# An interleaving copy without its small early write to the output

## The chip, the cores and the metric

One core of a Trainium2 chip runs the kernel. The metric is the device time of one execution in microseconds (us). Times quoted are medians of several executions. A ratio is computed otherwise: the mean time of one kernel's fast runs over the mean of the other's fast runs of the same rounds, so it is not quite the ratio of the medians.

## The reference

```python
# x, y: (32, 256, 1024) float32
result = np.zeros((batch, seq, dim * 2), dtype=np.float32)
result[..., 0::2] = x
result[..., 1::2] = y
```

Nothing is computed: 33.55 MB of x and as much of y are read, and 67.11 MB of output is written with the elements of the two inputs in turn.

## The kernel before

The kernel walks over 8 pairs of tiles of 128 partitions x 8192 elements (4 MB each). x and y are loaded from the SP queue; the vector engine copies x to the even and y to the odd places of an output tile, in halves of 4096 columns; the ACT queue stores each half (4 MB). Every pool has two buffers. The first x tile is loaded in two halves, one from each queue. Then comes the part that the change is about.

```python
xpool = ctx.enter_context(tc.tile_pool(name="xp", bufs=2))
ypool = ctx.enter_context(tc.tile_pool(name="yp", bufs=2))
opool = ctx.enter_context(tc.tile_pool(name="op", bufs=2))
# ... (cut)
wpool = ctx.enter_context(tc.tile_pool(name="wp", bufs=1))
zero = wpool.tile([16, 128], fp32, name="zero")
nc.vector.memset(zero, 0.0)
first = dataclasses.replace(of, offset=0, ap=[[2 * WL, 16], [1, 128]])

for lw in lwidths:                      # 8 times, lw = WL = 8192
    # ... (cut: xtile, ytile, xs, ys)
    if start == 0:
        for q, c in ((nc.sync, 0), (nc.scalar, lw // 2)):
            q.dma_start(out=xtile[:, c : c + lw // 2], in_=...)   # half of x
        nc.scalar.dma_start(out=first, in_=zero)                  # the small write
    else:
        nc.sync.dma_start(out=xtile, in_=xs)
    nc.sync.dma_start(out=ytile, in_=ys)
    # ... (cut: for each half of WS = 4096 columns)
        nc.vector.tensor_copy(out=otile[:, 0::2], in_=xsub)
        nc.vector.tensor_copy(out=otile[:, 1::2], in_=ysub)
        nc.scalar.dma_start(out=os_, in_=otile)
```

The small write puts 16 rows of 512 B of zeros, 8 KB in all, at places of the output that the first store overwrites later. It contributes nothing to the result.

Of the kernel before, what the change touches and what calls it, by code (L numbers as in the profile page):

```python
# [3 lines left out]

# [4 lines left out]


@with_exitstack
def _interleave(
    ctx: ExitStack,
    tc: tile.TileContext,
    x: bass.AP,
    y: bass.AP,
    out: bass.AP,
):
    nc = tc.nc  # L20
    P = 128

    total = 1
    for s in x.shape:
        total *= s

    WL = 8192
    WS = 4096

    xf = x.rearrange("b s d -> (b s d)")  # L30
    yf = y.rearrange("b s d -> (b s d)")
    of = out.rearrange("b s d -> (b s d)")

    fp32 = mybir.dt.float32
# [5 lines that stand above are left out]
    lwidths = [WL] * (total // P // WL)  # L40
    assert sum(lwidths) == total // P


    wpool = ctx.enter_context(tc.tile_pool(name="wp", bufs=1))
    zero = wpool.tile([16, 128], fp32, name="zero")
    nc.vector.memset(zero, 0.0)  # L46
    first = dataclasses.replace(of, offset=0, ap=[[2 * WL, 16], [1, 128]])

    start = 0
    for lw in lwidths:  # L50
        xtile = xpool.tile([P, WL], fp32, name="xtile")[:, :lw]
        ytile = ypool.tile([P, WL], fp32, name="ytile")[:, :lw]

        xs = dataclasses.replace(xf, offset=start, ap=[[lw, P], [1, lw]])
        ys = dataclasses.replace(yf, offset=start, ap=[[lw, P], [1, lw]])
        if start == 0:

            for q, c in ((nc.sync, 0), (nc.scalar, lw // 2)):
                q.dma_start(
                    out=xtile[:, c : c + lw // 2],  # L60
                    in_=dataclasses.replace(xf, offset=c, ap=[[lw, P], [1, lw // 2]]),
                )
            nc.scalar.dma_start(out=first, in_=zero)
        else:
            nc.sync.dma_start(out=xtile, in_=xs)
        nc.sync.dma_start(out=ytile, in_=ys)

        soff = 0
        while soff < lw:
            width = min(WS, lw - soff)  # L70
            otile = opool.tile([P, 2 * WS], fp32, name="otile")[:, : 2 * width]
            os_ = dataclasses.replace(
                of,
                offset=2 * start + 2 * soff,
                ap=[[2 * lw, P], [1, 2 * width]],
            )
            xsub = xtile[:, soff : soff + width]
            ysub = ytile[:, soff : soff + width]
# [3 lines that stand above are left out]
            soff += width  # L82

        start += P * lw
    assert start == total


def kernel(tc, x, y, out):
    nc = tc.nc
    _interleave(tc, x, y, out)  # L90
    tc.close()
    tc.compile()  # L92


    blocks = nc.main_func.blocks
    for engine in (mybir.EngineType.SP, mybir.EngineType.Activation):
        opening = blocks[0].instructions
        at, moved = next(
            (b, i)
            for b in blocks[1:]  # L100
            for i in b.instructions
            if i.engine == engine and i.opcode == "DMACopy"
        )
        assert not moved.sync_info.on_wait
        body = at.instructions
        body.remove(moved)
        gate = next(
            n
            for n, i in enumerate(opening)
            if i.engine == engine and i.opcode == "Drain"  # L110
        )
        opening.insert(gate, moved)
        at.instructions = body
        blocks[0].instructions = opening




    last = nc.main_func.blocks[-1]
    tail = last.instructions  # L120
    wait = tail[0]
    clear = next(n for n, i in enumerate(tail) if i.opcode == "ISA")
    assert wait.engine == mybir.EngineType.SP and wait.opcode == "Drain"
    assert wait.sync_info.on_wait and not wait.sync_info.on_update
    assert tail[clear].engine == mybir.EngineType.Pool
    last.instructions = [
        copy.replace(wait, engine=mybir.EngineType.Pool)
    ] + tail[clear:]


# [1 line left out]
_INS = ['x', 'y']  # L132
_OUTS = [((32, 256, 2048), 'float32')]


# [23 lines left out]
```

## Time and profile before

| | before |
|---|---|
| median of 3 runs | 315.84 us (315.67 to 316.25) |
| span of the profiled execution | 313.8 us |
| moved | 134.23 MB, 428 GB/s over the span |
| vector engine busy | 72.8 us (23%) |

The prediction below shows the totals, the rates by stretch and the start. Here is the chain that ended last, in order of time (start, length, what), from the first store on:

```profile
26.59 40.92 DMA out_dram<-otile
67.51 0.03 issue
67.53 0.02 DVEq L79
67.56 0.04 issue
67.60 2.30 DVE otile L79
```

Most of the chain (76% of the span) is a store on its way; the vector engine's 2.3 us pieces lie between. A store takes 13 to 41 us to land (half of them over 29 us) although its 4 MB need 9.7 us at 434 GB/s, because it shares the DMA engines with loads that are queued at the same time. The chain names who waits for whom; what limits the kernel is the sum of the bytes.

One more thing is needed to follow the argument. The trace holds a record of each DMA packet: queue, start, duration, size. In the large transfers a packet is 32 KB (16 KB in the first two half loads). I call *excess* what the records of the large packets in a stretch have over their usual 1213 ns (611 ns for 16 KB), counted where it is more than 12 ns, added up and divided by the 16 engines.

### The profile page before, as it was taken

To read this page: it belongs to the slowest core of one execution; us is meant where nothing else is said; L and a number is where in the kernel's file an instruction comes from. 1 tells how busy PE (TensorE), PEld (TensorE's weight loads), DVE (VectorE), ACT (ScalarE), POOL (GpSimd) and SP (SyncE) were. 2 spreads that over 40 slices of the span, in tenths; PEclk is the share of its full clock that TensorE was granted. 3 is DMA by queue.
4 is the path that set the end of the run, shared out by engine and by line. 5 is a ranking of instruction groups with operands and counts; after the bars stand their busy time and mean duration, and the time that the engine had idled before them with its cause. 6 is when DMAs were issued, how large, how long until landed. Compare 5 with 4: busy or idle time off the path is not lost.

```text
span 313.8 us, 141 instructions
## 1 busy us (share of the span) xinstructions
DVE 72.8 (23%) x33; POOL 0.2 (0%) x4
## 2 busy tenths in 40 slices
DVE  0523002231022410325003150031501305023500
POOL 0000000000000000000000000000000000000000
DMA  8999999999999999999999999999999999999997
GB/s 343 461 414 388 455 414 455 414 455 414 447 422 447 422 430 439 422 447 418 451 414 455 401 468 401 468 401 464 405 455 414 455 414 455 414 455 414 455 414 334
DMA packets 4784, 134.23 MB, mean 428 GB/s; under 512 B 544, under 2 KB 560, under 8 KB 560
## 3 DMA queue, kind: packets, MB, share of 16 engines
q10 hardware_dynamic: 2480, 69.22, 51.1%
q1 hardware_dynamic: 2304, 65.01, 48.4%
HBM read 67.11 MB, written 67.12 MB: 428 GB/s over the span
## 4 chain that ended last, share of the span: by engine, by line
DMA 83%; DVE 11%; DVEq 1%; issue 0%
DMA out_dram<-otile 76%; DMA ytile<-in_y_dram 7%; DVE otile L80 6%; DVE otile L79 5%; DVEq L92 1%; DVEq L79 0%
## 5 line engine op out<-in xcount | busy, mean ns | idle before, releaser
L79 DVE COPY otile<-xtile 128x4096 f32<-128x4096 f32 x16 | 36.6, 2295 | 184.7 <-DMA out_dram<-otile 174.1
L80 DVE COPY otile<-ytile 128x4096 f32<-128x4096 f32 x16 | 36.6, 2291 | 40.0 <-DMA ytile<-in_y_dram 40.0
L46 DVE MEMSET zero<- 16x128 f32 x1 | 0.2, 165 | 1.0 <-PEq L143 1.0
L143 POOL MEMSET const-bfloat16-1.0<- 128x1 bf16 x1 | 0.1, 101 | 0.0
L143 POOL MEMSET const-uint8-127<- 128x1 uint8 x1 | 0.1, 101 | 0.0
L143 POOL MEMSET const-float32-0.0<- 128x1 f32 x1 | 0.1, 98 | 0.2 <-issue 0.2
L143 POOL MEMSET const-float32-1.0<- 128x1 f32 x1 | 0.1, 98 | 0.0
## 6 DMA issues: line engine op xcount, KB each, us to landing
out_dram<-otile ACTq DMA_DIRECT2D x16, 4096.0 KB, 29.1
ytile<-in_y_dram SPq DMA_DIRECT2D x8, 4096.0 KB, 60.8
xtile<-in_x_dram SPq DMA_DIRECT2D x7, 4096.0 KB, 43.6
xtile<-in_x_dram SPq DMA_DIRECT2D x1, 2048.0 KB, 11.7
xtile<-in_x_dram ACTq DMA_DIRECT2D x1, 2048.0 KB, 13.4
out_dram<-zero ACTq DMA_DIRECT2D x1, 8.0 KB, 14.8
```

The lines of the kernel that those rows point to most:

```text
L46: nc.vector.memset(zero, 0.0)
L79: nc.vector.tensor_copy(out=otile[:, 0::2], in_=xsub)
L80: nc.vector.tensor_copy(out=otile[:, 1::2], in_=ysub)
L92: tc.compile()
L143: nc = _bacc.Bacc("TRN2", target_bir_lowering=False, num_devices=1)
```

## The change

Its intent: to leave out work that the result does not need.

```diff
-    wpool = ctx.enter_context(tc.tile_pool(name="wp", bufs=1))
-    zero = wpool.tile([16, 128], fp32, name="zero")
-    nc.vector.memset(zero, 0.0)
-    first = dataclasses.replace(of, offset=0, ap=[[2 * WL, 16], [1, 128]])
...
-            nc.scalar.dma_start(out=first, in_=zero)
```

## The prediction

> **What bounds the kernel now.** I read the page's totals first, then its slices in time, then the chain that ended last, and only then the start-up, because that is where the small write sits. The page of the kernel before, its totals, slices and queues:
>
> ```profile
> span 313.8 us, 141 instructions
> DVE 72.8 (23%) x33; POOL 0.2 (0%) x4
> ...
> DMA  8999999999999999999999999999999999999997
> GB/s 343 461 414 388 455 414 455 414 455 414 447 422 447 422 430 439 422 447 418 451 414 455 401 468 401 468 401 464 405 455 414 455 414 455 414 455 414 455 414 334
> DMA packets 4784, 134.23 MB, mean 428 GB/s; under 512 B 544, under 2 KB 560, under 8 KB 560
> ```
>
> The vector engine, the only engine that computes, is busy 23% of the time. The DMA row is at 9 (90% or more) in every slice but the first and the last. Of the packets, 544 are under 512 B; that is 34 transfers times 16 engines, the semaphore writes that end each transfer. 560 minus 544 leaves 16 packets of at least 512 B and under 2 KB: these are the small write, one packet for each engine. All else is in large packets. So the kernel moves 134.23 MB through 16 engines that hardly ever rest, and its time is bytes over rate plus what is lost at the ends.
>
> How level is that rate? The busy-time view in chosen stretches of the span (columns: stretch and its length, DVE, POOL, granted clock, DMA share, GB/s):
>
> ```profile
> 2.00:12.00 10.00, 0.28 (x1) 0.00 (x0) 1.00 1.05 447
> 12.00:16.00 4.00, 4.00 (x2) 0.00 (x0) 1.00 0.92 395
> 16.00:25.00 9.00, 3.15 (x3) 0.00 (x0) 1.00 1.05 455
> 25.00:29.00 4.00, 1.56 (x1) 0.00 (x0) 1.00 0.86 287
> 29.00:290.00 261.00, 59.00 (x26) 0.00 (x0) 1.00 1.00 434
> 290.00:312.00 22.00, 4.60 (x3) 0.00 (x0) 1.00 0.99 429
> 312.00:313.80 1.80, 0.00 (x0) 0.00 (x0) 1.00 0.01 0
> ```
>
> A packet is booked where it starts and lasts about 1.2 us, so short stretches swing by some 10% (447, 395 and 455 belong together). The reader is to see two things. From 29 to 290 us the engines are full at 434 GB/s. And there is one real dip, 287 GB/s between 25 and 29 us, just when the first large stores are issued. The trace's single packet records sharpen it: the 32 KB packets take 1213 ns nearly everywhere, but those that start between 25 and 28 us take up to 2046 ns, and the excess over 1213 ns adds up to 0.78 us for each engine (75 + 88 + 619 ns). This is the only loss after start-up, and it comes in spite of the small write having gone out before.
>
> The start in order of time:
>
> ```profile
> 1.00 0.17 DVE L46 MEMSET zero<- 16x128 f32 x1 [1.00 <-PEq L143]
> 1.20 0.39 ACTq L63 DMA_DIRECT2D out_dram<-zero  x1
> 1.30 0.52 SPq L65 DMA_DIRECT2D xtile<-in_x_dram  x1
> 1.87 0.47 SPq L66 DMA_DIRECT2D ytile<-in_y_dram  x1
> 11.72 4.50 DVE L79 COPY otile<-xtile 128x4096 f32<-128x4096 f32 x2 [10.55 <-DMA xtile<-in_x_dram]
> 16.24 0.33 SPq L65 DMA_DIRECT2D xtile<-in_x_dram  x1
> 22.06 4.49 DVE L80 COPY otile<-ytile 128x4096 f32<-128x4096 f32 x2 [5.85 <-DMA ytile<-in_y_dram]
> 24.39 2.56 ACTq L81 DMA_DIRECT2D out_dram<-otile  x2
> 26.59 0.33 SPq L66 DMA_DIRECT2D ytile<-in_y_dram  x1
> ```
>
> And the landing time of the small write, from the list of DMA issues:
>
> ```profile
> out_dram<-zero ACTq DMA_DIRECT2D x1, 8.0 KB, 14.8
> ```
>
> **What the Trainium skill says.** "DMA: Bandwidth & Descriptors", section Bandwidth, puts the ceiling of the 16 engines at 435 GB/s; the 434 GB/s of the long stretch agrees, so there is no slack for a smaller program to use. The same page, section Queues, rings and completion order, says each DMA engine takes turns between the queues that have work, a packet at a time. The trace agrees: the data of the small write starts at 13.7 us, and on each engine about 1.2 us passes between it and its semaphore write, the length of one 32 KB packet of the load queue. So the landing of 14.8 us is waiting in line behind loads, not cost. The page's Specifications give 512 B as the least size of a transfer at line rate; the small write's rows are just 512 B, and its packets took 27 ns each in the trace. I found no page that speaks of a first write to memory needing to be warmed; what the small write may have been for rests on the trace alone.
>
> **The change part by part.** Removed on the vector engine: one memset of 0.17 us at 1.00 us. That engine then idles until 11.72 us for x, so this is worth 0. Removed on the ACT queue: one issue of 0.39 us at 1.20 us. The next thing that queue does is the first store at 24.39 us; worth 0. While this issue ran, the SP queue's two neighbouring issues took 0.52 and 0.47 us against 0.33 us later, so they may get some 0.3 us shorter in sum. But they queue behind the first y load, whose data comes in until about 21 us; worth 0.
>
> Removed waits, from the built programs' order of instructions: the first store waited for the small write to land, because both write the same rows, and the second refill of y waited for it because it reuses its semaphore. The small write landed at 1.20 + 14.8 = 16.0 us. The first store was released by the first y copy, 22.06 + 2.29 = 24.35 us, and the refill by the second, at about 26.56 us. Both waits had been satisfied 8 us or more before; worth 0. Without the small write the eight DMA semaphores are dealt out one place earlier to everything that follows. I went through the waits of all later loads, stores and copies: each still waits for the same kind of earlier work, so this adds nothing.
>
> Removed from the DMA engines: on each, one packet of 27 ns and one semaphore write of 9 ns, together 0.036 us. This does lie on the path, since the engines are full. The first y load should land 0.04 us earlier, and all after it moves along. By bytes alone it would be 8192 B / 434 GB/s = 0.02 us. Nothing is added and nothing else moves: the order of instructions on every engine is otherwise the same. Sum: 315.84 - 0.04 = 315.80 us.
>
> **The rivals.** First, the small write warms something. If a first write costs a stall that the small one takes early, its removal moves that stall to the first large store. For it: the dip at 25 to 28 us shows that the start of stores can cost 0.78 us, and without a forerunner it could be worse. Against it: from 12 to 16 us all the large packets beside the small write keep 1213 ns, so the small write paid no stall that would now have to be paid elsewhere, and the dip came in spite of it. If it does warm something, I would expect the dip to grow by at most its own size again (a guess from that size), so 316.6 us.
>
> Second, the small write is itself part of what makes the dip, for instance through the wait or through a ring that it leaves part used. Then its removal gives back up to 0.78 us: 315.0 us. Against it: it was complete 9 us before the dip began. I rate it lower than the first.
>
> Third, the alternation of the two queues shifts its phase. The chain of waits repeats with a period of 38.7 us (store landings released the copies at 67.5, 106.2, 145.0 us, and so on) and the engines stay full whichever queue is served, so another phase changes landing times but not the sum: within 0.2 us either way.
>
> **The range and the chances.** Three runs of the kernel before span 315.67 to 316.25 us, so noise is about 0.3 us either way. To that I add the two forms of the dip: 0.8 us down if it disappears, 0.8 us up if it doubles, the latter a little more likely. That gives 315.80 us with a range from 315.1 to 316.7 us. Two per cent is 6.3 us, eight times the largest single effect that I can name; a fault of that size would have to make the DMA engines idle in every period. I give 0.985 to within 2%, 0.005 to faster and 0.01 to slower.
>
> **What would show each step right or wrong.** In the changed profile there should be 4752 packets (16 data and 16 semaphore packets fewer), with 528 under 512 B and as many under 2 KB; the memset and the small issue gone; the first y copies at about 22.0 us; the first stores issued at about 24.35 us; and 434 GB/s again from 29 to 290 us. The dip is the test of the rivals: an excess of 0.78 us for each engine means that the small write did nothing, clearly more means that it warmed something, none means that it caused the dip. I would be wrong if the engines showed gaps after 29 us, if the first store were issued later than before, or if the loss at the very start (the first packets of x) differed, which nothing in the change touches.

## The result

The time stayed the same: 315.62 us (315.51 to 315.99, 6 runs) against 315.64 us for the kernel before (6 runs); ratio 0.9999, 95% interval 0.9987 to 1.0012.

The page of the changed kernel, the same rows as before, and the queue of instruction fetches:

```profile
span 313.8 us, 138 instructions
DVE 72.6 (23%) x32; POOL 0.2 (0%) x4
...
DMA  8999999999999999999999999999999999999997
GB/s 340 462 405 397 451 418 443 426 443 426 434 434 422 447 418 451 414 455 405 464 401 468 401 468 401 464 405 464 405 464 405 455 414 443 426 443 426 443 426 334
DMA packets 4753, 134.22 MB, mean 428 GB/s; under 512 B 529, under 2 KB 529, under 8 KB 529
...
q14 instruction: 1, 0.00, 0.0%
```

The span is the same to a tenth of a microsecond. The 16 packets between 512 B and 2 KB are gone, and so are 16 semaphore packets: the count under 512 B is 529 and not the predicted 528 only because one instruction fetch fell into this profile. The DMA row is as full as it was.

The start in order of time:

```profile
0.92 0.33 SPq L59 DMA_DIRECT2D ytile<-in_y_dram  x1
1.30 0.52 SPq L58 DMA_DIRECT2D xtile<-in_x_dram  x1
1.88 0.50 SPq L59 DMA_DIRECT2D ytile<-in_y_dram  x1
11.75 4.50 DVE L72 COPY otile<-xtile 128x4096 f32<-128x4096 f32 x2 [11.75 <-DMA xtile<-in_x_dram]
...
22.08 4.50 DVE L73 COPY otile<-ytile 128x4096 f32<-128x4096 f32 x2 [5.83 <-DMA ytile<-in_y_dram]
24.41 2.56 ACTq L74 DMA_DIRECT2D out_dram<-otile  x2
```

The first y copy starts at 22.08 us against 22.06 before, the first store is issued at 24.41 against 24.39. The memset and the small issue are gone, and nothing has moved into their place. The chain that ended last has the same pieces; its line for the first stores, the store that was 40.92 us on its way before:

```profile
26.61 40.97 DMA out_dram<-otile
```

The busy time by stretch (length, DVE, POOL, clock, DMA share, GB/s), changed kernel:

```profile
25.00:29.00 4.00, 1.58 (x1) 0.00 (x0) 1.00 0.99 344
24.00:32.00 8.00, 2.58 (x2) 0.00 (x0) 1.00 1.00 389
29.00:290.00 261.00, 58.95 (x26) 0.00 (x0) 1.00 1.00 434
```

And the eight-microsecond stretch of the kernel before:

```profile
24.00:32.00 8.00, 2.56 (x2) 0.00 (x0) 1.00 1.00 389
```

The row from 25 to 29 us reads 344 GB/s where before it read 287, as if the dip had shrunk. It has not: a packet is booked where it starts, and 16 packets on one side of a border are 16 x 32768 B / 4 us = 131 GB/s. Over 24 to 32 us both kernels have 389 GB/s. The packet records settle it: 0.76 us of excess for each engine (32 + 125 + 601 ns) against 0.78 us before.

### The profile page after: what moved, and what is told of

Same layout as the page of the kernel before. It is cut to its first block, busy times and chain, and to the rows that moved or that the text cites. A ratio compares the mean times of both kernels' runs of the same rounds, so it can differ in the third digit from the quotient of the medians.

```text
span 313.8 us, 138 instructions
## 1 busy us (share of the span) xinstructions
DVE 72.6 (23%) x32; POOL 0.2 (0%) x4
## 4 chain that ended last, share of the span: by engine, by line
DMA 83%; DVE 11%; DVEq 1%; issue 0%
DMA out_dram<-otile 76%; DMA ytile<-in_y_dram 7%; DVE otile L73 6%; DVE otile L72 5%; DVEq L85 1%; DVEq L72 0%
```

## The experiments

Two questions were left. The expected effect, 0.036 us, is far below what a timing resolves (the interval above is 0.4 us either way), so the cost of a small write had to be shown enlarged. And the dip at the first stores had to be tied to its cause, since both rivals rested on it. All kernels but *tiny_no_wait*, which is the kernel before with one line changed, are edits of the changed kernel. All gave the correct result.

**repeat**: the changed kernel unaltered, five rounds.

> The changed kernel again, five rounds. Theory (the small write costs each DMA engine 36 ns and warms nothing): ratio to before between 0.999 and 1.001, the excess of the stretched packets between 25 and 28 us again 0.7 to 0.8 us for each engine, as in the first profiles with (0.78) and without (0.76) the small write. Rival (the small write warms the store path): excess above 0.9 us and a ratio above 1.001.

Measured: 315.67 us against 315.67, ratio 0.9996 (0.9983 to 1.0008); excess at the first stores 0.74 us. As the theory has it, on another occasion.

**dose_512**: 128 packets of 512 B for each engine in place of one, issued on the load queue just ahead of the first y load.

```diff
+    zero = wpool.tile([128, 128], fp32, name="zero")
+    nc.vector.memset(zero, 0.0)
+    many = dataclasses.replace(
+        of, offset=2 * (total - P * WL), ap=[[2 * WL, 128], [1024, 16], [1, 128]]
+    )
...
+            nc.sync.dma_start(
+                out=many, in_=zero.unsqueeze(1).to_broadcast([128, 16, 128])
+            )
```

> The cost of the small write multiplied: 2048 rows of 512 B, 128 for each DMA engine in place of 1, spread over all 128 partitions, on the load queue ahead of the first y load, to rows that the last stores overwrite. Theory (each packet occupies its engine for 27 ns, and the engines are full, so all of it reaches the end): 128 x 27 ns = 3.5 us more, 319.1 us. By bytes alone 1.05 MB / 434 GB/s = 2.4 us, 318.0 us. If small writes hide beside the loads: 315.6 us.

Measured: 319.54 us against 315.55, ratio 1.0125 (1.0110 to 1.0140). That is 3.9 us more (3.5 to 4.4), or 31 ns (27 to 35) for each of the 128 packets. All 2048 small packets are there, and their records have a median of 27 ns. The page's packet row and the start in order of time:

```profile
DMA packets 6816, 135.27 MB, mean 426 GB/s; under 512 B 544, under 2 KB 2592, under 8 KB 2592
```

```profile
1.21 0.62 SPq L64 DMA_DIRECT2D out_dram<-zero  x1
1.88 11.15 SPq L69 DMA_DIRECT2D ytile<-in_y_dram  x1
...
13.07 0.58 SPq L68 DMA_DIRECT2D xtile<-in_x_dram  x1
...
26.17 4.50 DVE L83 COPY otile<-ytile 128x4096 f32<-128x4096 f32 x2 [9.66 <-DMA ytile<-in_y_dram]
```

The y copy starts at 26.17 us, 4.1 us later than in the kernel before, and the end is 3.9 us later. The late copy alone would prove little (in x1_on_act, below, it comes 8 us later at no cost); the late end does: what these small writes take from full engines is not hidden and not given back. By bytes alone the loss would be 2.4 us, which the interval excludes, and so it does "hidden". The packets' own 3.46 us lie at the interval's lower edge. In the records the large packets show 1.0 us more excess for each engine than in the kernel before in the first 20 us (0.23 in the first 4 us, 0.77 from 9 us on, before, beside and after the small packets) and 0.19 us less at the first stores (0.60), so 0.84 us more in sum. On the other side, packet records overlap (more than 16 under way) by 0.41 us for each engine more than before, nearly all of it beside the small packets. 3.46 + 0.84 - 0.41 gives the measured 3.9 us. So the 31 ns for a packet hold some 7 ns that other packets lost; that the small ones caused this loss is likely and not shown, and no run takes the two apart.

**tiny_no_wait**: the small write stays and goes elsewhere, so that the first store does not wait for it.

```diff
-    first = dataclasses.replace(of, offset=0, ap=[[2 * WL, 16], [1, 128]])
+    first = dataclasses.replace(of, offset=2 * (total - P * WL), ap=[[2 * WL, 16], [1, 128]])
```

> The small write stays where it was but goes to rows of the last tile, so the first store no longer waits for it: one part of the change alone. Theory (that wait had been met 8 us before): same time, ratio 0.999 to 1.001, first stores issued at 24.4 us as before, the dip again 0.7 to 0.8 us. Rival (the wait is what costs or delays): the first stores move by over 0.2 us.

Measured: 315.68 us against 315.55, ratio 1.0007 (0.9992 to 1.0022). The first stores were issued at 24.43 us, 0.04 us from before. So the removed wait was worth nothing. The excess at the first stores was 0.55 us, under the expected 0.7: the dip varies more from one execution to another than I had put down.

**late_tiny**: the small write moved to 8 us before the first stores, by taking its data from the loaded x.

```diff
+            if start == 0 and soff == WS:
+                nc.vector.tensor_copy(out=zero[:, :128], in_=xtile[:16, soff : soff + 128])
+                nc.scalar.dma_start(out=late, in_=zero)      # 16 rows of 512 B of the last tile
```

> The small write (8 KB) moved to just before the first stores: issued at about 16.3 us on an idle queue. Theory (small writes warm nothing): dip 0.7 to 0.8 us for each engine after the first store's issue, time 315.6 to 315.8 us. Rival (a forerunner has to come shortly before): dip under 0.4 us, time near 315.2 us.

Measured: 315.63 us against 315.55, ratio 1.0001 (0.9984 to 1.0018); excess at the first stores 0.64 us, between the two expectations and nearer to the theory. The start of it:

```profile
16.52 0.36 ACTq L82 DMA_DIRECT2D out_dram<-zero  x1
22.27 4.50 DVE L83 COPY otile<-ytile 128x4096 f32<-128x4096 f32 x2 [5.78 <-DMA ytile<-in_y_dram]
24.60 2.56 ACTq L84 DMA_DIRECT2D out_dram<-otile  x2
```

A forerunner 8 us before the stores, on a queue that stood idle, changes neither the time nor, clearly, the dip.

**late_tiny_read**: as late_tiny, with a load of 8 KB in place of the write.

```diff
-                nc.scalar.dma_start(out=late, in_=zero)
+                nc.scalar.dma_start(out=zero, in_=dataclasses.replace(xf, offset=0, ap=[[WL, 16], [1, 128]]))
```

> As late_tiny, but 8 KB are loaded instead of written: one 512 B packet for each engine on the idle ACT queue at about 16.3 us. In late_read, with 15 KB rows on 16 partitions, the stretched packets came at the load and none came at the first stores. If any use of the queue in the read direction were enough for that, the excess at the first stores falls under 0.4 us here. If the size of the disturbance did it, the dip stays at 0.6 to 0.8 us. Time 315.5 to 315.8 us in either case.

Measured: 315.72 us against 315.71, ratio 1.0001 (0.9982 to 1.0020); excess 0.69 us at the first stores. The direction of a small forerunner does not matter either.

**early_15k**: the small write in its old place in the queue, thirty times as large, to rows of the last tile. Its longer memset (3.26 us) delays its issue from 1.20 to 5.08 us; its packets start at 13.9 us, as the small ones did (13.7).

```diff
+    zero = wpool.tile([16, 3840], fp32, name="zero")
+    late = dataclasses.replace(of, offset=2 * (total - P * WL), ap=[[2 * WL, 16], [1, 3840]])
+    nc.vector.memset(zero, 0.0)
...
+            nc.scalar.dma_start(out=late, in_=zero)
```

> The small write thirty times as large (16 rows of 15 KB, still one packet for each engine, in the same place in the queue, to rows that the last tile's stores overwrite). Theory: pure cost on full engines, about 15360/32768 of 1213 ns = 0.57 us, so 316.2 us if before is 315.6; the dip at 25 to 28 us stays at 0.7 to 0.8 us. Rival (a write large enough warms): the dip shrinks below 0.4 us and its stall shows at 13 to 16 us instead, or is gone.

Measured: 316.93 us against 315.67, ratio 1.0042 (1.0025 to 1.0059), so 1.3 us more where 0.57 was expected. The excess at the first stores was 0.58 us, and 0.17 us appeared from 12 to 15 us, most of it in the write's own packets (573 to 972 ns). The dip stayed within the scatter of the other kernels (0.55 to 0.89 us), so a larger forerunner does not remove it. The time was missed because I had reckoned with the mean engine. The last stretches, kernel before:

```profile
312.00:313.00 1.00, 0.00 (x0) 0.00 (x0) 1.00 0.01 0
313.00:314.00 1.00, 0.00 (x0) 0.00 (x0) 1.00 0.00 0
```

and early_15k:

```profile
312.00:313.00 1.00, 0.00 (x0) 0.00 (x0) 1.00 0.23 98
313.00:314.00 1.00, 0.00 (x0) 0.00 (x0) 1.00 0.08 33
```

98 and 33 GB/s over 1 us are three packets and one packet of 32 KB. Only these four start after 312 us, in a kernel whose other engines are done. By the packet records the engines' last semaphore writes come on average at 313.16 us against 312.56 before, 0.60 us later, close to the 0.57 reckoned, but the last of them at 314.32 against 312.85, 1.47 us later. The time is that of the slowest engine. Why a write of 16 long rows sets one or two engines back more than the others stays open.

**late_write** and **late_read**: the same 15 KB rows, written or loaded on the ACT queue, issued at 18.18 us (late_write, 6 us before the first stores) and at 16.35 us (late_read; 8 us were meant, but the stores came late, so it was 11.6 us). The edits are those of late_tiny and late_tiny_read with 3840 columns; late_write copies all of them on the vector engine first (2.1 us).

> The 15 KB-per-engine write is issued at about 18.5 us, when the ACT queue has stood idle for 6 us, 6 us before the first store. It tells what the dip belongs to. If the dip belongs to the first write or to the restart of an idle queue, packets stretch at about 20 us and the dip at 25 to 28 us shrinks. If it belongs to the full-size first store, nothing stretches at 20 us and 0.7 to 0.8 us stays at 25 to 28 us. Time: 316.2 us in all cases where the dip only moves, 315.4 us if it is gone.

> As late_write, but a load of the same size on the same ACT queue, issued at about 16.4 us. If the dip is the restart of an idle queue whatever the direction, packets stretch at about 18 us and the dip at 25 to 28 us shrinks; if it belongs to stores, it stays at 0.7 to 0.8 us and nothing stretches at 18 us. Time 316.2 us (0.57 us of engine time more than before).

Measured: late_write 317.02 us, ratio 1.0036 (1.0020 to 1.0052), excess 0.03 us from 19 to 22 us and 0.89 us at the first stores. So the first write of some size after an idle time stretches nothing, and the first full-size store still does. The time missed the expected 316.2 for the same reason as in early_15k: the engines end 0.63 us later on average, the last 1.53 us later.

late_read 318.21 us, ratio 1.0078 (1.0065 to 1.0092), 2 us over what was expected. Here the large packets between 19 and 25 us took up to 3.3 us, 1.5 us of excess for each engine (and 0.8 us more in the 15 KB packets themselves, against the 573 ns that they took in late_write), and no packet was stretched beyond 12 ns at the first stores, which were issued at 27.92 us. This load to 16 partitions therefore cost far more than its bytes (no run loads as much to more partitions), and after it the dip is missing. This is one profile; late_tiny_read shows that it is not the direction alone. Why this disturbance takes the dip's place stays open.

**swap**: all loads from the ACT queue, all stores from SP.

```diff
-        for q, c in ((nc.sync, 0), (nc.scalar, lw // 2)):
+        for q, c in ((nc.scalar, 0), (nc.sync, lw // 2)):
...                                      # and nc.sync <-> nc.scalar in the other three issues
```

> No small write; the two issuing queues trade places: all loads from the ACT queue, all stores from SP. It asks whether the dip belongs to the queue or to the start of the stores. If to stores, the excess after the first store's issue is 0.7 to 0.8 us again and the time 315.6 us; if to the ACT queue, it is gone and the time is 314.9 us.

Measured: 315.58 us against 315.55, ratio 1.0006 (0.9991 to 1.0021); excess 0.75 us after the first store's issue at 24.35 us. The dip does not belong to the ACT queue.

**x1_on_act**: the second x load goes through the ACT queue, which delays the first y and so the first stores.

```diff
-            nc.sync.dma_start(out=xtile, in_=xs)
+            q = nc.scalar if start == P * WL else nc.sync
+            q.dma_start(out=xtile, in_=xs)
```

> No small write; the second x load goes through the ACT queue, so that this queue is busy with useful 32 KB packets until shortly before the first stores. If the dip needs a queue that has stood idle, it falls under 0.4 us and the time is about 315.0 us; if it comes with the first stores whatever the queue did before, the excess stays at 0.6 to 0.8 us and the time is 315.6 us, since the bytes are the same.

Measured: 315.58 us against 315.71, ratio 0.9994 (0.9978 to 1.0010). The first stores came 8 us later:

```profile
30.34 4.50 DVE L74 COPY otile<-ytile 128x4096 f32<-128x4096 f32 x2 [14.33 <-DMA ytile<-in_y_dram]
32.67 2.57 ACTq L75 DMA_DIRECT2D out_dram<-otile  x2
```

In this kernel no packet is stretched from 25 to 33 us, and 0.83 us of excess lies between 34 and 37 us. So the dip follows the first stores here too, 8 us later, and a queue kept busy until shortly before does not prevent it. It also shows that 8 us of delay in the first copies cost nothing, as long as the engines have loads to do.

The packet records say one thing more of the dip. In the kernel before, all 26 stretched packets are loads, on the SP queue; they start from 25.85 to 27.70 us, and the first packet of the store starts only at 29.18 us, 4.8 us after its issue. It is so in all eleven profiles that have the dip (in swap the loads are on the ACT queue, and so are the stretched packets): loads are slow between the issue of the first store and its first packet, which comes 4.2 to 5.0 us after it (after that, no profile has more than 0.01 us of excess before 40 us). It is not the store's own data that is slow. In every run the first store is issued 2.3 us after the first y copy starts, so none tells the one event from the other as what the dip follows.

Put together, by the excess at the first stores, one profile each: with a small write 0.78 (before), 0.55 (tiny_no_wait) and 0.64 us (late_tiny); without any forerunner 0.76 (changed), 0.74 (repeat), 0.75 (swap) and 0.83 us (x1_on_act). The first group is lower by some 0.1 us on average, but its own scatter is 0.2 us, and no ratio of times shows a difference. An effect of that size can be neither shown nor excluded here. No version beat the two kernels; removing the dip altogether would be worth at most about 0.8 us, 0.25%.

## Why the prediction was right

*The bound.* DMA engines full at 434 GB/s from 29 to 290 us: confirmed by the same 434 afterwards, and by dose_512, where work added to the engines came out at the end.

*The parts worth nothing.* The memset and the issue: their removal shows nowhere. The wait of the first store: tiny_no_wait takes it away alone, ratio 1.0007 with the interval spanning 1. The other order of the semaphores: no new wait in the changed kernel's chain, which reads as before.

*The part on the path.* 0.036 us was the sum. One profile cannot show it: the first y copies came 0.02 us later, not 0.04 us earlier, which fits the 0.05 us more that the first packets of x happened to lose (excess from 1 to 4 us: 0.68 against 0.63 us; 0.54 to 0.79 us over all profiles). The enlarged dose gave 31 ns (27 to 35) for a packet, some 7 ns of it lost by other packets, which is of the size of the 27 ns that the step used; the semaphore write's 9 ns are read from the records and not tested by themselves. That the measured medians differ by 0.02 us is no support for 0.036: the interval is 0.4 us either way, and any effect well below that would have come out so.

*The rivals.* "It warms something" asked for a larger dip without the small write: 0.76 and 0.74 us against 0.78. "It is part of the dip" asked for a smaller one: the same numbers. Both fall as effects on the dip of more than about 0.2 us. The dip comes in the loads, after the issue of the first full-size stores and before their packets, on either queue (swap) and wherever they are (x1_on_act), but not after late_read's disturbance; its mechanism was not found, and that the first y copy brings it was not tested. The third rival, a shifted phase, was tried most strongly by x1_on_act, whose loads and stores meet quite differently, at a ratio of 0.9994.

*The signs of being wrong.* No gaps came after 29 us. Two of the signs did come, too small to mean anything: the first store was issued 0.02 us later than before, and the loss at the very start differed by 0.05 us; both lie within the scatter between profiles of the same kernel (the repeat has its first store at 24.46 us and 0.67 us from 1 to 4 us).

*Two details were wrong.* The neighbouring SP issues did not get shorter: 0.52 and 0.50 us, against 0.52 and 0.47. It was not the small write's issue that made them long. And the row from 25 to 29 us was a poor measure of the dip: it moved from 287 to 344 GB/s while the packet records moved by 0.02 us.

## What to carry to other kernels

When the DMA engines are full from end to end, ask of a transfer first how long it occupies its engines, and then whether all engines alike: the last one to finish sets the time (early_15k, 1.3 us where the mean said 0.6). Where its issue, its wait and its landing lie did not matter here while other transfers filled the time. An effect below the noise can be settled by enlarging it a hundred times and dividing, if what is enlarged keeps its form (more packets of 512 B, not longer ones), and by moving the suspected event to see whether its trace follows. Before you keep a warm-up trick, take it out and look for the loss that it was to prevent.

## What the Trainium skill lacked or had wrong

- "DMA: Bandwidth & Descriptors", section Specifications, gives 512 B as the least transfer at line rate. Here a 512 B packet occupied its engine for 27 ns, which is 19 GB/s, against 27 GB/s for a 32 KB packet (32768 B in 1213 ns): 70% of the rate. By the clock, 128 of them cost 31 ns each.
- No page that I found mentions the loss at the first full-size stores: 0.55 to 0.89 us for each engine in eleven of the twelve profiles, from 1.0 to 1.6 us after the first store's issue on, in the packets of the loads, whichever queue had the stores. It was absent in one (late_read).
- "Perfetto Trace Analysis", section DMA Instruction — HWDGE, says an issue's recorded window lasts until its descriptors are generated, and that engines may start before that if more are generated than the buffer holds. In dose_512 the issue of an ordinary y load, behind one of 2048 rows, took 11.15 us in place of 0.33. This fits a full buffer, and also the wait for the lock on the descriptor generator, which that section counts into the window; no record tells which. The page gives no size for the buffer and does not warn that the next issue on the queue is blocked for so long.
- No page that I found says that a transfer of few rows can leave single engines behind: with 16 rows of 15 KB written (early_15k) the engines ended 0.60 us later on average and the last one 1.47 us; the cause is open.
- The same DMA page's section Bandwidth was right in its ceiling of 435 GB/s, against 434 measured. Its note that for transfers between HBM and SBUF the HBM side (about 358 GB/s) binds did not hold here, where all transfers are such and one core works: they ran at 434 GB/s. (The same section says elsewhere that about 358 is what each core gets when both stream.)
